# A hybrid decoder on one core: the time mixing's gate is projected ahead of the attention's keys and values, and small products of a step are kept together

## The chip, the core and the metric

The kernel runs on one core of one Trainium2 chip. The metric is the device time of one execution in microseconds (us); a kernel's time is the median of its runs. TensorE (PE) multiplies matrices, VectorE (DVE), ScalarE (ACT) and GpSimd (POOL) work on elements, SyncE (SP) starts the loads of the weights. Each engine executes its own list of instructions in order.

## The reference

Two decoder layers of width 2048 over 256 positions, batch 1, float32. One input projection feeds three token mixers and their gates; their outputs are joined, projected and added to the residual under a layer norm.

```python
u = x @ w_in                     # columns split among the mixers and their gates
# A) short convolution: b * conv3(c * h) * silu(gate)
# B) latent attention: 8 heads, keys/values from ukv (rank 256), queries from uq (rank 512)
# C) time mixing (RWKV-7), 8 heads x 64, gate u_rg:
def step(state, inp):
    r_t, w_t, k_t, v_t, a_t, b_t = inp
    sa = einsum('bhvk,bhk->bhv', state, a_t)
    state = state * w_t + sa * b_t + v_t * k_t
    return state, einsum('bhvk,bhk->bhv', state, r_t)
yf = scan(step)                  # then a norm per head
ym = mean(yf, -1); yv = mean(square(yf - ym), -1)
y = (yf - ym) * rsqrt(yv + eps) * gn_g + gn_b
y = (y + bonus) * silu(gate)
x = LayerNorm(alpha * x + concat(A, B, C) @ w_out)
```

## The kernel before

Every large product is made three times, from a high and a low part of both operands (`mm3`, lines 332 to 334). Weights come in blocks of 1 MB by SP; ACT casts the high part `hi_*` and DVE subtracts to get the low part `lo_*`. A group of the input projection (`in_group`) is 192 matmuls of 128x256 into two accumulators `u_*` of the pool `pp`, which has four. The groups are named k, r, a, v (time mixing), cq (queries' rank), cc, ch, cb, cg (convolution), rg (the time mixing's gate) and mg0, mg1 (the attention's gate). A layer runs the groups of `MAIN`, then `mla_kv` (accumulators pkn and pvt, evicted as kn, vs, vt), `mla_q` (pqn, pqp), then the groups of `LATE`, then the output projection `po`. `plan` lists the weight loads in the same order.

The three mixers are generators. After each small block of a projection, `tick` lets them issue their next steps, so that their small products stand between large ones. The time mixing works in four chunks c of 64 positions: GpSimd and DVE scale keys into `bk` (GpSimd the upper 64 rows, "hi"), TensorE forms the products `pg`, DVE masks them into `gs`, a triangular solve follows (pz, px), and then the recurrence: for each chunk prh from the state, `rhs` on DVE, pu, its copy `uvt` on DVE and ACT, pst, the new state `st` on DVE. `py` gives the outputs of two chunks. When both are there, the norm runs: copies of y on ACT, mean `gm`, difference, squares `gsq`, variance `gv`, a reciprocal root `grs` in small steps, product. Then the transposes `pt`, the activation `yy`, bonus, gate, and the cast `mr` that the output projection reads.

A scheduler puts the instructions of each engine in order when the program is built, by its own estimate of times and by priorities; `tc.high_priority(AHEAD)` moves a step ahead. A tile of a pool is claimed in the order in which the program asks for it (`s8`, nine tiles of 8 KB a partition, holds kn, vs, qn and mr among others).

Of the kernel before, what the change touches and what calls it, by code (L numbers as in the profile page):

```python
# [10 lines left out]
F32 = mybir.dt.float32  # L11
# [98 lines left out]
def hybrid_layers(ctx: ExitStack, tc: tile.TileContext, x, positions, xT, w_in, w_out, w_uq, w_ukv, par, wa_in, gb_in,  # L110
# [34 lines left out]
    def after(inst, earlier):  # L145

        tc.add_manual_dep(inst.ins, earlier.ins.name,
                          mybir.DependencyInfo(mybir.DependencyClass.NoSync, mybir.DependencyReason.DATA),
                          reason="loads no earlier than needed")


    cs = cp.tile([P, K_W], F32, tag="cs", name="cs")
# [186 lines left out]
        for i, src in enumerate((hi, lo)):  # L339
            T.matmul(o, ones[:, which * P:which * P + P], src, start=i == 0, stop=i == 1)  # L340

    MAIN, LATE, ORDER = ("k", "r", "a", "v", "cq", "cc", "ch", "cb", "cg"), ("rg", "mg0", "mg1"), (0, 12, 4, 8)

    def plan():

# [64 lines left out]
    def gate(ps2, name):  # L410

        th = sm.tile([P, 2, S], F32, tag="b2", name=f"th_{name}", bufs=3)
        with tc.high_priority(AHEAD):
            A.activation(th, ps2, AF.Tanh, scale=0.5)
        sg = sm.tile([P, 2, S], F32, tag="b2", name=f"sg_{name}", bufs=3)
        with tc.high_priority(AHEAD):
            V.scalar_tensor_tensor(sg, th, 1.0, ps2, ALU.add, ALU.mult)
        return sg


    UNITS = [(h, c) for c in range(4) for h in range(HEADS)]
# [130 lines left out]
    def rwkv_scale(l, pq, st):  # L552
        col = pq["col"]
        kx, kkn, rx, tha, pe, pinv = (st[k] for k in ("kx", "kkn", "rx", "tha", "pe", "pinv"))
        kp = s4(f"kp{l}")
        for b in range(4):
            A.activation(kp[:, b, :], tha[:, b, :], AF.Identity, scale=col(pq["hk"] + b), bias=col(pq["ok"] + b))
        V.tensor_tensor(kp, kp, kx, ALU.mult)
        V.tensor_scalar(tha, tha, 0.5, 0.5, ALU.mult, ALU.add)
        yield  # L560
        bk = s8(f"bk{l}", (P, 16, P))
        ar = s8(f"ar{l}", (P, 4, 2, S))
        c16 = lambda a: a.rearrange("p b (c t) -> p (b c) t", t=64)
        lo_, hi_ = halves
        G.tensor_tensor(bk[hi_, :, 0:64], c16(kp)[hi_], c16(pinv)[hi_], ALU.mult)
        for b in range(4):
            V.scalar_tensor_tensor(chunks(ar[:, b, 0, :]), chunks(kkn[:, b, :]), -1.0,
                                   pe[:, b * 4:(b + 1) * 4, 0:64], ALU.mult, ALU.mult)
            if b % 2:
                yield  # L570
        V.tensor_tensor(kkn, kkn, tha, ALU.mult)
        G.tensor_tensor(bk[hi_, :, 64:128], c16(kkn)[hi_], c16(pinv)[hi_], ALU.mult)  # L572
        yield
        V.tensor_tensor(bk[lo_, :, 0:64], c16(kkn)[lo_], c16(pinv)[lo_], ALU.mult)
        V.tensor_tensor(bk[lo_, :, 64:128], c16(kp)[lo_], c16(pinv)[lo_], ALU.mult)
        yield
        for b in range(4):
            V.tensor_tensor(chunks(ar[:, b, 1, :]), chunks(rx[:, b, :]), pe[:, b * 4:(b + 1) * 4, 1:65], ALU.mult)
        yield
        st["ar"], st["bk"], st["kp"] = ar, bk, kp  # L580

    def rwkv_v(l, pq, st, uv):
        rx = st["rx"]
# [13 lines left out]
    def rwkv_products(l, st):  # L597

        ar, bk = st["ar"], st["bk"]
        gs = [s8(f"gs{l}_{i}", (P, 2, HEADS, P)) for i in range(2)]  # L600
        for c in range(4):
            cc = slice(c * 64, (c + 1) * 64)
            pg = [pm.tile([P, 4, P], F32, tag="m", name=f"pg{l}_{c}_{par}") for par in range(2)]
            for b in range(4):
                for par in range(2):
                    r = halves[par]
                    T.matmul(pg[par][:, b, :].rearrange("p (q t) -> p q t", q=2), bk[r, b * 4 + c, :], ar[r, b, :, cc],
                             start=True, stop=True)
            for par in range(2):
                gv = gs[c // 2][:, c % 2].rearrange("p (b q) t -> p b q t", q=2)[:, :, par, :]  # L610
                st["mark"] = V.tensor_tensor(gv, pg[par], gmask.unsqueeze(1).to_broadcast([P, 4, P]), ALU.mult)
            yield
        st["gs"] = gs
        col, rx, kp = params[l]["col"], st["rx"], st["kp"]
        for b in range(4):
            V.scalar_tensor_tensor(rx[:, b, :], rx[:, b, :], col(Q_RK + b), kp[:, b, :], ALU.mult, ALU.mult)
        yield
        st["rh"], st["rl"] = c4(f"rh{l}", dt=F32R), c4(f"rl{l}", dt=F32R)
        split_in(st["rh"], st["rl"], rx)

    def rwkv_inverse(l, st):
# [40 lines left out]
        yield  # L662
        for par in range(2):
            r = slice(par * 64, par * 64 + 32)
            V.transpose(xt1[r].rearrange("p c b t -> p (c b) t"), xq[r, :, :, 0:32].rearrange("p c b t -> p (c b) t"))
        yield
        zs = sm.tile([P, 16, 32], F32, tag="s", name=f"zs{l}")
        quarters = [(slice(par * 64, par * 64 + 32), slice(par * 64 + 32, par * 64 + 64)) for par in range(2)]
# [1 line left out]
        for c in range(4):  # L670
            for b in range(4):
                for par, (ra, rb) in enumerate(quarters):
                    T.matmul(pz[par][rb, c * 4 + b, :], gs[c // 2][ra, c % 2, 2 * b + par, 32:64], xt1[ra, c, b, :],
                             start=True, stop=True)
        for par, (ra, rb) in enumerate(quarters):
            V.tensor_copy(zs[rb], pz[par][rb])
        yield
        px = [pm.tile([P, 16, 32], F32, tag="m", name=f"px{l}_{par}") for par in range(2)]
        for c in range(4):
            for b in range(4):  # L680
                for par, (ra, rb) in enumerate(quarters):
                    T.matmul(px[par][ra, c * 4 + b, :], zs[rb, c * 4 + b, :], xq[rb, c, b, 32:64], start=True, stop=True)
        for par, (ra, rb) in enumerate(quarters):
            V.tensor_copy(xq[ra, :, :, 32:64].rearrange("p c b t -> p (c b) t"), px[par][ra])
        yield
        st["xq"] = xq

    def rwkv_pairs(l, st):
# [14 lines left out]
        for b2 in range(2):  # L703
            pv = pm.tile([P, 2, 4, 64], F32, tag="m", name=f"pv{l}_{b2}")
            for bb in range(2):
                for c in range(4):
                    for par in range(2):
                        r, o = halves[par], halves[1 - par]
                        T.matmul(pv[o, bb, c, :], vx[r, b2 * 2 + bb, c * 64:(c + 1) * 64], ident[r, r],
                                 start=True, stop=True)  # L710
            for bb in range(2):
                for par in range(2):
                    o = halves[1 - par]
                    A.copy(hv(uvt, o, b2 * 2 + bb, par), pv[o, bb])
            yield
        st["uvt"], st["bkt"] = uvt, bkt
        qs = s4(f"qs{l}", (P, 4, 4, 64))
        for c2 in range(2):
            pq_ = pm.tile([P, 2, 4, 64], F32, tag="m", name=f"pq{l}_{c2}")
            for cc in range(2):  # L720
                c = c2 * 2 + cc
                for b in range(4):
                    for par in range(2):
                        h = 2 * b + par
                        kr = halves[1 - par]
                        T.matmul(pq_[halves[par], cc, b, :], gs[c // 2][kr, c % 2, h, 0:64], uvt[kr, c, h, :],
                                 start=True, stop=True)
# [4 lines left out]
    def rwkv_chain(l, st):  # L732
# [2 lines left out]
        rs = halves  # L735
        state = None

        def out(c2, states):

            py = [pm.tile([P, 4, 64], F32, tag="m", name=f"py{l}_{c2}_{par}") for par in range(2)]  # L740
            for par in range(2):
                for b in range(4):
                    h = 2 * b + par
                    for i, state in enumerate(states):
                        T.matmul(py[par][halves[i], b, :], gs[c2][:, i, h, 64:128], uvt[:, 2 * c2 + i, h, :],
                                 start=b == 0, stop=state is None, skip_group_check=True)
# [12 lines left out]
        for c in range(4):  # L759
# [10 lines left out]
                yield  # L770
            pu = pm.tile([P, 4, 64], F32, tag="m", name=f"pu{l}_{c}")
            for b in range(4):
                for par in range(2):
                    T.matmul(pu[rs[par], b, :], xq[rs[par], c, b, :], rhs[rs[par], b, :], start=True, stop=True)
            for par in range(2):
                dst = uvt[:, c].rearrange("p (b q) t -> p b q t", q=2)[rs[par], :, par, :]
                if par == 0:
                    V.tensor_copy(dst, pu[rs[par]])
                else:
                    A.copy(dst, pu[rs[par]])  # L780
            yield
            if c < 3:
                pst = pm.tile([P, 4, 64], F32, tag="m", name=f"pst{l}_{c}")
                for b in range(4):
                    for par in range(2):
                        h = 2 * b + par
                        T.matmul(pst[rs[par], b, :], bkt[:, c, h, :], uvt[:, c, h, :], start=True, stop=True)
                new = slot("st", f"st{l}_{c}", (P, 4, 64), 2)
                pc_ = pe[:, c::4, 64:65].to_broadcast([P, 4, 64])
                if state is None:  # L790
# [3 lines left out]
                    V.tensor_tensor(new, new, pc_, ALU.mult)  # L794
            before.append(state)
            if c % 2:
                out(c // 2, before[-2:])
            if c < 3:
                state = new
            yield  # L800
# [117 lines left out]
    def mla_kv(l, st):  # L918
# [4 lines left out]
        for h2 in range(4):  # L923
# [3 lines left out]
            for k in range(2):  # L927
# [5 lines left out]
                for t in range(2):  # L933
                    ts_ = slice(t * P, t * P + P)
                    mm3(pv[:, t, :].rearrange("p (b c) -> p b c", b=2), hi[:, k, ts_], lo[:, k, ts_], wv(whi), wv(wlo),
                        k == 0 and t == 0, k == 1)
            with tc.high_priority(AHEAD):
                A.copy(kn[:, 2 * h2:2 * h2 + 2, :], pk)
                of, pv = slice(2 * h2, 2 * h2 + 2), pv.rearrange("p t (b c) -> p t b c", b=2)
                split_in(vs[:, 0, of, :], vs[:, 1, of, :], pv[:, 0])  # L940
# [5 lines left out]
    def mla_q(l, st):  # L946
# [3 lines left out]
        for g in range(4):  # L950
# [3 lines left out]
            for kc in range(4):  # L954
# [3 lines left out]
                    mm3(pn[:, b, :], whi[:, k, b * P:b * P + P], wlo[:, k, b * P:b * P + P],  # L958
                        hi[:, kc, :], lo[:, kc, :], kc == 0 and b == 0, kc == 3)
                mm3(pe_, whi[:, k, 256:384], wlo[:, k, 256:384], hi[:, kc, :], lo[:, kc, :], kc == 0, kc == 3)  # L960
            with tc.high_priority(AHEAD):
# [387 lines left out]
```

## Time and profile before

| | us |
|---|---|
| median of 3 runs | 933.12 |
| lowest, highest | 930.76, 933.73 |
| the profiled execution | 930.57 |
| its span in the trace | 928.8 |
| PE busy in it | 910.0 |
| DVE, ACT, POOL busy | 682.1, 468.2, 42.0 |

Times in the rows of the profile are measured from the start of the span, and lie 1.8 us within the execution's own time. A row of the list of waits has the waiting engine and its product, the line, what was waited for, then the total in us, how often, and the longest. A row of the stretches has the bounds, the length, then the busy time of PE, PE's weight loads, DVE, ACT and POOL with the number of instructions, the granted clock of TensorE, the share of busy DMA engines, and GB/s. A row of the chain or the timeline has start, duration and what ran. A row of a tile has shortest, median and longest duration in ns, and the first and last start. The mean clock was 0.996 of full speed.

### The profile page before, as it was taken

What the parts mean: (1) busy time and instruction counts of PE and PEld (TensorE: products, weight loads), DVE (VectorE), ACT (ScalarE), POOL (GpSimd) and SP (SyncE); (2) the same over time, 40 slices, a digit from 0 to 9 for tenths busy, and PEclk for the clock granted to TensorE, in tenths of its full rate; (3) what the DMA queues carried; (4) which work ended last, traced back from release to release, by engine and by line L of the source; (5) the groups of instructions that cost most, each with busy time, mean ns of one, the idle gap of its engine ahead of it and who ended that gap; (6) DMA issues with size and microseconds to landing.
All of it is one profiled execution on the core that took longest, in us unless ns stands there. A gap on an engine that the chain in (4) does not pass through costs nothing.

```text
span 928.8 us, 18409 instructions
## 1 busy us (share of the span) xinstructions
PE 910.0 (98%) x7719; PEld 867.6 (93%) x7719; DVE 682.1 (73%) x1132; ACT 468.2 (50%) x716; POOL 42.0 (5%) x47
## 2 busy tenths in 40 slices
PE   8999999999999999999999999999999999999996
PEld 7999989999989999888899999899998999998895
DVE  6687898886569875666766688988854898755665
ACT  6656535543455675434346465463434657754430
POOL 1210130000000000000010001300000000000000
PEclk9999999999999999999999999999999999999999
DMA  8965355354425435964665544463544363259542
GB/s 295 288 200 181 137 187 165 127 183 137 163 98 188 176 127 170 345 208 149 204 227 182 178 148 175 148 203 136 183 117 137 135 225 141 97 175 371 177 136 90
DMA packets 47523, 165.12 MB, mean 178 GB/s; under 512 B 13446, under 2 KB 22198, under 8 KB 32582
## 3 DMA queue, kind: packets, MB, share of 16 engines
q1 hardware_dynamic: 39680, 150.35, 47.4%
q10 hardware_dynamic: 5072, 9.57, 3.3%
q0 software_dynamic: 2688, 4.03, 1.6%
q8 instruction: 60, 0.98, 0.4%
q14 instruction: 23, 0.19, 0.1%
HBM read 158.61 MB, written 5.32 MB: 177 GB/s over the span
## 4 chain that ended last, share of the span: by engine, by line
PE 89%; DMA 3%; DVE 3%; POOL 2%; ACT 1%; issue 1%; SPq 0%; DVEq 0%; ACTq 0%
PE po L332 6%; PE po L333 6%; PE po L334 6%; PE u_mg L334 3%; PE u_mg L333 3%; PE u_mg L332 3%; PE u_ch L332 2%; PE u_cg L333 2%; PE u_cc L332 2%; PE u_cg L332 2%; POOL bk L572 2%; PE u_cg L334 2%; PE u_rg L334 2%; PE u_rg L333 2%; PE u_rg L332 2%; PE u_cb L334 2%
## 5 line engine op out<-in xcount | busy, mean ns | idle before, releaser
L136 DVE TENSOR_TENSOR lo_wo<-w_wo,hi_wo 128x1024 fp32r<-128x1024 f32 x57 | 69.4, 1223 | 51.7 <-ACT hi_wo L136 50.3
L136 ACT CAST hi_wo<-w_wo 128x1024 fp32r<-128x1024 f32 x57 | 59.8, 1053 | 80.8 <-PE po L334 56.0
L333 PE MATMUL u_mg<-x,hi_mg 128*128 128x256 f32 x256 | 72.6, 283 | 0.0
L334 PE MATMUL u_mg<-x,lo_mg 128*128 128x256 f32 x256 | 72.6, 283 | 0.0
L332 PE MATMUL u_mg<-x,hi_mg 128*128 128x256 f32 x256 | 72.4, 283 | 0.0
L136 DVE TENSOR_TENSOR lo_mg<-w_mg,hi_mg 128x1024 fp32r<-128x1024 f32 x32 | 39.1, 1223 | 18.5 <-ACT hi_mg L136 18.4
L333 PEld LDWEIGHTS u_mg<-x,hi_mg 128*128 128x128 f32 x256 | 49.1, 192 | 0.0
L334 PEld LDWEIGHTS u_mg<-x,lo_mg 128*128 128x128 f32 x256 | 49.0, 192 | 0.0
L332 PEld LDWEIGHTS u_mg<-x,hi_mg 128*128 128x128 f32 x256 | 49.0, 192 | 0.0
L333 PE MATMUL po<-lo_wo,ma 128*128 128x512 f32 (+1 forms) x128 | 46.4, 362 | 0.0
L334 PE MATMUL po<-hi_wo,ma 128*128 128x512 f32 (+1 forms) x128 | 46.4, 362 | 0.0
L332 PE MATMUL po<-hi_wo,ma 128*128 128x512 f32 (+1 forms) x128 | 45.9, 363 | 0.0
L136 ACT CAST hi_mg<-w_mg 128x1024 fp32r<-128x1024 f32 x32 | 33.6, 1049 | 22.1 <-PE u_mg L333 13.3
L332 PE MATMUL u_ch<-x,hi_ch 128*128 128x256 f32 x128 | 37.0, 289 | 0.0
L333 PE MATMUL u_cg<-x,hi_cg 128*128 128x256 f32 x128 | 37.0, 289 | 0.0
L334 PE MATMUL u_cq<-x,lo_cq 128*128 128x256 f32 x128 | 37.0, 289 | 0.0
L332 PE MATMUL u_k<-x,hi_k 128*128 128x256 f32 x128 | 36.5, 290 | 0.4 <-ACT hi_k L136 0.3
L333 PE MATMUL u_cq<-x,hi_cq 128*128 128x256 f32 x128 | 36.7, 287 | 0.0
L332 PE MATMUL u_cc<-x,hi_cc 128*128 128x256 f32 x128 | 36.7, 289 | 0.0
L332 PE MATMUL u_cq<-x,hi_cq 128*128 128x256 f32 x128 | 36.6, 286 | 0.0
L332 PE MATMUL u_cg<-x,hi_cg 128*128 128x256 f32 x128 | 36.6, 286 | 0.0
L334 PE MATMUL u_k<-x,lo_k 128*128 128x256 f32 x128 | 35.6, 285 | 0.9 <-DVE lo_k L136 0.9
(424 smaller groups left out, 3417.2 us busy)
## 6 DMA issues: line engine op xcount, KB each, us to landing
w_wo<-in_w_out_dram SPq DMA_DIRECT2D x24, 1024.0 KB, 6.1
w_mg<-in_w_in_dram SPq DMA_DIRECT2D x16, 1024.0 KB, 4.8
w_r<-in_w_in_dram SPq DMA_DIRECT2D x8, 1024.0 KB, 6.4
w_a<-in_w_in_dram SPq DMA_DIRECT2D x8, 1024.0 KB, 4.9
w_v<-in_w_in_dram SPq DMA_DIRECT2D x8, 1024.0 KB, 4.9
w_cq<-in_w_in_dram SPq DMA_DIRECT2D x8, 1024.0 KB, 4.8
w_cc<-in_w_in_dram SPq DMA_DIRECT2D x8, 1024.0 KB, 4.9
w_ch<-in_w_in_dram SPq DMA_DIRECT2D x8, 1024.0 KB, 5.2
```

The source lines that it names most:

```text
L136: inst = call(*args, **kwargs)
L332: m = T.matmul(o, lh, rh, start=first, stop=False, skip_group_check=True)
L333: T.matmul(o, lh, rl, start=False, stop=False, skip_group_check=True)
L334: T.matmul(o, ll, rh, start=False, stop=last, skip_group_check=True)
L572: G.tensor_tensor(bk[hi_, :, 64:128], c16(kkn)[hi_], c16(pinv)[hi_], ALU.mult)
```

## The change

The gate group rg goes from `LATE` to the end of `MAIN`, and with it its four loads. The first matmul of a small product now waits in the order (without a semaphore) for the step's last input, so that the product's matmuls are not spread (`gather`; the two halves of the partitions are taken in the order 1, 0 in pg, pu and pst). GpSimd's two products of 64x1024 into bk become eight of 64x256. `gate` writes into the tile of the tanh. The evictions of mla_kv and mla_q get the priority 4000 in place of 1500.

```diff
+EVICT = 4000
+    def gather(m, earlier):
+        for e in earlier:
+            after(m, e)
-    MAIN, LATE, ORDER = ("k", "r", "a", "v", "cq", "cc", "ch", "cb", "cg"), ("rg", "mg0", "mg1"), (0, 12, 4, 8)
+    MAIN, LATE, ORDER = ("k", "r", "a", "v", "cq", "cc", "ch", "cb", "cg", "rg"), ("mg0", "mg1"), (0, 12, 4, 8)
...
-        sg = sm.tile([P, 2, S], F32, tag="b2", name=f"sg_{name}", bufs=3)
-            V.scalar_tensor_tensor(sg, th, 1.0, ps2, ALU.add, ALU.mult)
-        return sg
+            V.scalar_tensor_tensor(th, th, 1.0, ps2, ALU.add, ALU.mult)
+        return th
...
-        G.tensor_tensor(bk[hi_, :, 0:64], c16(kp)[hi_], c16(pinv)[hi_], ALU.mult)
+        def chunk(c, src, at):
+            cc = slice(c * 64, c * 64 + 64)
+            return G.tensor_tensor(bkc[hi_, :, c, at:at + 64], src[hi_, :, cc], pinv[hi_, :, cc], ALU.mult)
+        for c in range(3):
+            chunk(c, kp, 0)
...
-        G.tensor_tensor(bk[hi_, :, 64:128], c16(kkn)[hi_], c16(pinv)[hi_], ALU.mult)
+        for c in range(4):
+            if c == 2:
+                chunk(3, kp, 0)
+            ready_.append([chunk(c, kkn, 64)])
...
-                for par in range(2):
+                for par in (1, 0):
+                    if b == 0 and par:
+                        gather(m, st["ready"][c])
...
-                for par in range(2):
-                    T.matmul(pu[rs[par], b, :], xq[rs[par], c, b, :], rhs[rs[par], b, :], start=True, stop=True)
+                for par in (1, 0):
+                    m = T.matmul(pu[rs[par], b, :], xq[rs[par], c, b, :], rhs[rs[par], b, :], start=True, stop=True)
+                    if c == b == 0 and par:
+                        gather(m, [st["xq1"]])
...
-            with tc.high_priority(AHEAD):
+            with tc.high_priority(EVICT):
                 A.copy(kn[:, 2 * h2:2 * h2 + 2, :], pk)
```

The same form of `gather` stands in pz, px, pq, pst and py. The built program has 6523 rows on TensorE where it had 6539, the same matmuls.

How the order moves, first on TensorE in layer 0 around the transposes of the time mixing's output. Before, they stand behind the gate's last matmuls (u_rg) and the first of the attention's gate (u_mg), and ahead of the attention's scores (sc):

```order
L333 MATMUL u_rg_1_3524<-x_3_85,hi_rg_12_2_3743 128x256
L334 MATMUL u_rg_1_3524<-x_3_85,lo_rg_12_2_3744 128x256
L332 MATMUL u_mg_0_4047<-x_0_82,hi_mg_0_0_3873 128x256
L333 MATMUL u_mg_0_4047<-x_0_82,hi_mg_0_0_3873 128x256
L334 MATMUL u_mg_0_4047<-x_0_82,lo_mg_0_0_3874 128x256
L828 MATMUL pt_0_3281<-cs,y_2671 128x128 x4
L828 MATMUL pt_1_3347<-cs,y_2671 128x128 x4
L1006 MATMUL sc_0_3603<-kn_3097,qn_3289 128x128
```

Between py_1's last matmul and these stood 295 rows, the rest of the queries and the whole gate. The same place now, from py_1's last matmul on:

```order
L781 MATMUL py_1_1_3055<-st_2_2971,ar_1321 64x64
L339 MATMUL pvt_1_3443<-lo_ukv_1_0_0_3397,hkv_1653 128x256
L340 MATMUL pvt_1_3443<-hi_ukv_1_0_0_3396,hkv_1653 128x256
L338 MATMUL pvt_1_3443<-hi_ukv_1_0_0_3396,hkv_1653 128x256
L339 MATMUL pvt_1_3443<-lo_ukv_1_0_0_3397,hkv_1653 128x256
L340 MATMUL pvt_1_3443<-hi_ukv_1_0_0_3396,hkv_1653 128x256
L862 MATMUL pt_0_3244<-cs,y_2677 128x128 x4
L862 MATMUL pt_1_3286<-cs,y_2677 128x128 x4
L338 MATMUL pkn_2_3478<-hkv_1653,hi_ukv_2_0_0_3438 128x256
```

Five matmuls of the values stand between py_1 and pt_0; the keys pkn_2 follow. The second layer has the same rows.

ScalarE, the evictions of the keys in layer 0. Before, kn<-pkn_0 and kn<-pkn_1 stand behind a copy of the recurrence (uvt) and weight casts:

```order
L136 COPY uvt_1928<-pu_1_2767 64x4x64
L136 CAST hi_uq_0_0_2_3246<-w_uq_0_0_3240 128x2x384
L136 COPY kn_3097<-pkn_0_3106 128x512
L136 COPY kn_3097<-pkn_1_3153 128x512
L136 COPY y_2671<-py_0_0_2824 128x4x64
```

Now they stand behind the norm and the output of the time mixing:

```order
L137 COPY y_2677<-py_1_1_3055 128x4x64
L137 CAST hi_uq_0_0_2_3514<-w_uq_0_0_3508 128x2x384
L137 ACTIVATE gsq_3134<-y_2677 128x1024
L137 ACTIVATE yy_3243<-pt_0_3244,pars 128x256 x2
L137 ACTIVATE yy_3243<-pt_1_3286,pars 128x256 x2
L137 CAST mr_3372<-yy_3243 128x512
L137 COPY kn_3391<-pkn_0_3400 128x512
L137 CAST vs_3393<-pvt_0_3401 128x256
L137 COPY kn_3391<-pkn_1_3442 128x512
```

The squares gsq, the activations yy and the first cast mr have moved ahead of kn<-pkn_0.

VectorE, the norm in layer 0, which stood spread among weight splits. Now one split lo_uq stands between its first two links and the rest follow one another:

```order
L137 TENSOR_REDUCE gm_3130<-y_2677 128x16
L137 TENSOR_TENSOR lo_uq_0_0_2_3515<-w_uq_0_0_3508,hi_uq_0_0_2_3514 128x2x384
L137 TENSOR_SCALAR gm_3130<-gm_3130 128x16
L137 TENSOR_TENSOR y_2677<-y_2677,gm_3130 128x1024
L137 TENSOR_REDUCE gv_3164<-gsq_3134 128x16
L137 TENSOR_SCALAR gv_3164<-gv_3164 128x16
L137 TENSOR_SCALAR grs_3166<-gv_3164 128x16
L137 TENSOR_TENSOR nr_g_3168<-grs_3166 128x16
```

Before, 44 rows lay between gm and the product with grs; now 16 do, and but for lo_uq and a MEMSET they are the norm's own.

More of the change, by code (lines that the diff above doesn't have):

```diff
@@ L564, in rwkv_scale @@
         lo_, hi_ = halves
-        G.tensor_tensor(bk[hi_, :, 0:64], c16(kp)[hi_], c16(pinv)[hi_], ALU.mult)
+        bkc = bk.rearrange("p (b c) t -> p b c t", c=4)
+        def chunk(c, src, at):
[3 more added lines that the diff above has]
+            chunk(c, kp, 0)
         for b in range(4):
@@ L571, in rwkv_scale @@
         V.tensor_tensor(kkn, kkn, tha, ALU.mult)
-        G.tensor_tensor(bk[hi_, :, 64:128], c16(kkn)[hi_], c16(pinv)[hi_], ALU.mult)
+        ready_ = []
+        for c in range(4):
+            if c == 2:
+                chunk(3, kp, 0)
+            ready_.append([chunk(c, kkn, 64)])
         yield
@@ L577, in rwkv_scale @@
         for b in range(4):
-            V.tensor_tensor(chunks(ar[:, b, 1, :]), chunks(rx[:, b, :]), pe[:, b * 4:(b + 1) * 4, 1:65], ALU.mult)
+            v = V.tensor_tensor(chunks(ar[:, b, 1, :]), chunks(rx[:, b, :]), pe[:, b * 4:(b + 1) * 4, 1:65], ALU.mult)
         yield
-        st["ar"], st["bk"], st["kp"] = ar, bk, kp
+        st["ar"], st["bk"], st["kp"], st["ready"] = ar, bk, kp, [r + [v] for r in ready_]
     def rwkv_v(l, pq, st, uv):
@@ L604, in rwkv_products @@
             for b in range(4):
-                for par in range(2):
+                for par in (1, 0):
                     r = halves[par]
-                    T.matmul(pg[par][:, b, :].rearrange("p (q t) -> p q t", q=2), bk[r, b * 4 + c, :], ar[r, b, :, cc],
-                             start=True, stop=True)
+                    m = T.matmul(pg[par][:, b, :].rearrange("p (q t) -> p q t", q=2), bk[r, b * 4 + c, :],
+                                 ar[r, b, :, cc], start=True, stop=True)
+                    if b == 0 and par:
+                        gather(m, st["ready"][c])
             for par in range(2):
@@ L611, in rwkv_products @@
                 st["mark"] = V.tensor_tensor(gv, pg[par], gmask.unsqueeze(1).to_broadcast([P, 4, P]), ALU.mult)
+            if c < 2:
+                st["ready"][c + 2].append(st["mark"])
             yield
@@ L664, in rwkv_inverse @@
             r = slice(par * 64, par * 64 + 32)
-            V.transpose(xt1[r].rearrange("p c b t -> p (c b) t"), xq[r, :, :, 0:32].rearrange("p c b t -> p (c b) t"))
+            t1 = V.transpose(xt1[r].rearrange("p c b t -> p (c b) t"), xq[r, :, :, 0:32].rearrange("p c b t -> p (c b) t"))
         yield
@@ L672, in rwkv_inverse @@
                 for par, (ra, rb) in enumerate(quarters):
-                    T.matmul(pz[par][rb, c * 4 + b, :], gs[c // 2][ra, c % 2, 2 * b + par, 32:64], xt1[ra, c, b, :],
-                             start=True, stop=True)
+                    m = T.matmul(pz[par][rb, c * 4 + b, :], gs[c // 2][ra, c % 2, 2 * b + par, 32:64],
+                                 xt1[ra, c, b, :], start=True, stop=True)
+                    if c == b == par == 0:
+                        gather(m, [t1])
         for par, (ra, rb) in enumerate(quarters):
-            V.tensor_copy(zs[rb], pz[par][rb])
+            z1 = V.tensor_copy(zs[rb], pz[par][rb])
         yield
@@ L681, in rwkv_inverse @@
                 for par, (ra, rb) in enumerate(quarters):
-                    T.matmul(px[par][ra, c * 4 + b, :], zs[rb, c * 4 + b, :], xq[rb, c, b, 32:64], start=True, stop=True)
+                    m = T.matmul(px[par][ra, c * 4 + b, :], zs[rb, c * 4 + b, :], xq[rb, c, b, 32:64],
+                                 start=True, stop=True)
+                    if c == b == par == 0:
+                        gather(m, [z1])
         for par, (ra, rb) in enumerate(quarters):
-            V.tensor_copy(xq[ra, :, :, 32:64].rearrange("p c b t -> p (c b) t"), px[par][ra])
+            st["xq1"] = V.tensor_copy(xq[ra, :, :, 32:64].rearrange("p c b t -> p (c b) t"), px[par][ra])
         yield
@@ L713, in rwkv_pairs @@
                     o = halves[1 - par]
-                    A.copy(hv(uvt, o, b2 * 2 + bb, par), pv[o, bb])
+                    st["uv1"] = A.copy(hv(uvt, o, b2 * 2 + bb, par), pv[o, bb])
             yield
@@ L725, in rwkv_pairs @@
                         kr = halves[1 - par]
-                        T.matmul(pq_[halves[par], cc, b, :], gs[c // 2][kr, c % 2, h, 0:64], uvt[kr, c, h, :],
-                                 start=True, stop=True)
+                        m = T.matmul(pq_[halves[par], cc, b, :], gs[c // 2][kr, c % 2, h, 0:64], uvt[kr, c, h, :],
+                                     start=True, stop=True)
+                        if cc == b == par == 0:
+                            gather(m, [st["uv1"]])
             A.copy(qs[:, c2 * 2:c2 * 2 + 2], pq_)
@@ L736, in rwkv_chain, with out @@
         state = None
-        def out(c2, states):
+        def out(c2, states, moved):
             py = [pm.tile([P, 4, 64], F32, tag="m", name=f"py{l}_{c2}_{par}") for par in range(2)]
@@ L744, in out @@
                     for i, state in enumerate(states):
-                        T.matmul(py[par][halves[i], b, :], gs[c2][:, i, h, 64:128], uvt[:, 2 * c2 + i, h, :],
-                                 start=b == 0, stop=state is None, skip_group_check=True)
+                        m = T.matmul(py[par][halves[i], b, :], gs[c2][:, i, h, 64:128], uvt[:, 2 * c2 + i, h, :],
+                                     start=b == 0, stop=state is None, skip_group_check=True)
+                        if par == b == i == 0:
+                            gather(m, moved)
             for b in range(4):
@@ L772, in rwkv_chain @@
             for b in range(4):
-                for par in range(2):
-                    T.matmul(pu[rs[par], b, :], xq[rs[par], c, b, :], rhs[rs[par], b, :], start=True, stop=True)
+                for par in (1, 0):
+                    m = T.matmul(pu[rs[par], b, :], xq[rs[par], c, b, :], rhs[rs[par], b, :], start=True, stop=True)
+                    if c == b == 0 and par:
+                        gather(m, [st["xq1"]])
+            moved = []
             for par in range(2):
@@ L777, in rwkv_chain @@
                 if par == 0:
-                    V.tensor_copy(dst, pu[rs[par]])
+                    moved.append(V.tensor_copy(dst, pu[rs[par]]))
                 else:
-                    A.copy(dst, pu[rs[par]])
+                    moved.append(A.copy(dst, pu[rs[par]]))
             yield
@@ L784, in rwkv_chain @@
                 for b in range(4):
-                    for par in range(2):
+                    for par in (1, 0):
                         h = 2 * b + par
-                        T.matmul(pst[rs[par], b, :], bkt[:, c, h, :], uvt[:, c, h, :], start=True, stop=True)
+                        m = T.matmul(pst[rs[par], b, :], bkt[:, c, h, :], uvt[:, c, h, :], start=True, stop=True)
+                        if b == 0 and par:
+                            gather(m, moved)
                 new = slot("st", f"st{l}_{c}", (P, 4, 64), 2)
@@ L796, in rwkv_chain @@
             if c % 2:
-                out(c // 2, before[-2:])
+                out(c // 2, before[-2:], moved)
             if c < 3:
@@ L960, in mla_q @@
                 mm3(pe_, whi[:, k, 256:384], wlo[:, k, 256:384], hi[:, kc, :], lo[:, kc, :], kc == 0, kc == 3)
-            with tc.high_priority(AHEAD):
+            with tc.high_priority(EVICT):
                 A.copy(qn[:, 2 * g:2 * g + 2, :], pn)
```

## The prediction

> **What bounds the kernel now.** First the busy times, then the chain of work that ended last, then the waits of TensorE, then busy time by stretch.
>
> ```profile
> PE 910.0 (98%) x7719; PEld 867.6 (93%) x7719; DVE 682.1 (73%) x1132; ACT 468.2 (50%) x716; POOL 42.0 (5%) x47
> PE 89%; DMA 3%; DVE 3%; POOL 2%; ACT 1%; issue 1%; SPq 0%; DVEq 0%; ACTq 0%
> PE prh L767 <- DVE st L136: 3.5, 2, 1.7
> PE pg L607 <- POOL bk L572: 2.7, 2, 1.4
> 110.00:140.00 30.00, 28.63 (x239) 27.33 (x237) 27.95 (x36) 12.13 (x15) 10.65 (x2) 0.94 0.52 178
> 250.00:280.00 30.00, 28.09 (x372) 26.33 (x371) 18.25 (x35) 15.69 (x31) 0.40 (x1) 1.00 0.28 98
> 280.00:300.00 20.00, 20.00 (x169) 20.00 (x168) 19.57 (x37) 13.11 (x19) 0.80 (x3) 1.00 0.60 212
> ```
>
> TensorE (PE) is busy 910.0 of 928.8 us and executes its list in order, so the kernel is its list plus its waits. All waits together are 18.8 us; of these the change can reach only two kinds inside a layer, prh on st (3.5 us in two layers) and pg on bk (2.7 us). Whatever the change gains by taking waits away is therefore under some 7 us; what it may lose has no such bound. The stretch 280 to 300 is to be remembered: TensorE idles for nothing there, while VectorE (DVE) works for 19.57 of 20 us on a chain that nobody waits for yet.
>
> **The gate moved ahead: what loses its cover.** In each layer py closes the recurrence, a norm over y follows on ScalarE (ACT) and DVE, and the transposes pt need its result. Rows of the first layer, from the timeline and the tile views:
>
> ```profile
> 270.21 1.08 PE py L745 x28
> 271.29 0.62 PE py L752 x32
> 272.97 0.65 ACT L136 COPY y<-py 128x256 f32<-128x256 f32 x2
> 274.25 1.21 DVE L136 TENSOR_REDUCE gm<-y 128x16 f32<-128x1024 f32 x1
> 275.38 0.95 DVE L136 TENSOR_TENSOR lo_uq<-w_uq,hi_uq 128x768 fp32r<-128x768 f32 x1
> 276.24 0.17 DVE L136 TENSOR_SCALAR gm<-gm 128x16 f32<-128x16 f32 x1
> 278.63 1.23 DVE L136 TENSOR_TENSOR y<-y,gm 128x1024 f32<-128x1024 f32 x1
> 279.95 1.06 ACT L136 ACTIVATE gsq<-y 128x1024 f32<-128x1024 f32 x1 [1.37 <-DVE y L136]
> 284.42 1.22 DVE L136 TENSOR_REDUCE gv<-gsq 128x16 f32<-128x1024 f32 x1
> 290.46 0.17 DVE L136 TENSOR_SCALAR gv<-gv 128x16 f32<-128x16 f32 x1
> 293.15 0.17 DVE L136 TENSOR_SCALAR grs<-gv 128x16 int32<-128x16 int32 x1
> 302.42 0.18 DVE L136 SCALAR_TENSOR_TENSOR nr_g<-nr_g,gv 128x16 f32<-128x16 f32 x1
> 302.63 0.18 DVE L136 SCALAR_TENSOR_TENSOR grs<-nr_g,grs 128x16 f32<-128x16 f32 x1
> 303.86 1.22 DVE L136 TENSOR_TENSOR y<-y,grs 128x1024 f32<-128x1024 f32 x1
> L828 PE MATMUL pt<-cs,y x16: 272/273/273, 307.3 to 766.4; 128*128 128x128 f32 x16
> ```
>
> Before, py ends at 271.9 and pt starts at 307.3. The 35 us between are filled by the rest of the attention's queries and by the whole gate projection u_rg, so the chain may take its time (it ends at 305.1, with weight splits between its links). In the changed order the gate stands ahead of the keys and values, and between py_1 and pt_0 TensorE has five matmuls left (the first order listing under the change). A matmul of this form issues every 0.12 us (row below), so the cover is 0.6 us.
>
> The chain without strangers, by the rows: two copies of y 0.65; mean 1.21; one lo_uq, which stands in the changed DVE order inside the chain and takes 0.87 until the next starts; 0.17; difference 1.23; squares 1.06; variance 1.22; two small operations 0.34; nine steps of the reciprocal root, which follow each other at 0.21 (302.42 to 302.63), 1.9; product 1.22. That is 9.87 us. Five hand-overs between engines at about 0.1 (278.63 + 1.23 = 279.86, and gsq starts at 279.95) add 0.5, and the end of the last py matmuls 0.1. 10.5 − 0.6 leaves a wait of **9.9 us** at pt_0 in each layer; the order is the same in the second. Bounds: 8.6, if lo_uq slips into the square's 1.06 and hops cost nothing; 10.9, if each hop costs twice.
>
> A second wait follows. In the changed ACT order the first eviction of the keys, kn<-pkn_0, stands behind the four yy<-pt and the first mr<-yy, and pkn_2 needs the accumulator that it frees.
>
> ```profile
> L136 ACT ACTIVATE yy<-pt,pars x8: 557/566/576, 308.5 to 768.1; 128x256 f32<-128x256 f32 x8
> L136 DVE TENSOR_TENSOR yy<-yy,bon x4: 689/690/691, 310.4 to 769.9; 128x512 f32<-128x512 f32 x4
> L136 DVE SCALAR_TENSOR_TENSOR yy<-sg_rg,yy x4: 687/688/690, 313.0 to 772.3; 128x512 f32<-128x512 f32 x4
> L136 ACT CAST mr<-yy x4: 605/606/606, 314.4 to 774.1; 128x512 fp32r<-128x512 f32 x4
> L136 ACT COPY kn<-pkn x8: 586/587/592, 252.1 to 716.4; 128x512 f32<-128x512 f32 x8
> ```
>
> From the end of pt_0: 2 × 0.57 + 0.69 + 0.69 + 0.61 + 0.59 = 3.7, hops 0.3, less the 0.45 in which pt_1 still runs: **3.5 us**. It is 2.9 if the hops vanish and pt takes longer, 4.1 if the next eviction, behind the second mr (0.61), is also waited for. Giving the evictions a higher priority does not help, since mr stands ahead of kn. The last weight splits in the way (hi_ukv, hi_uq) I cost at nothing: they are done while TensorE waits. So are the gate's four weight loads, which SP now issues ahead of those of ukv and uq: in 250 to 280 the DMA engines were 0.28 busy, and the stream that the queue carries is the same one, reordered.
>
> **The clock.** The first layer's short wait at pg was followed by slow matmuls:
>
> ```profile
> 129.20:132.60 3.40, 3.40 (x21) 3.18 (x21) 1.55 (x4) 2.16 (x4) 0.00 (x0) 0.50 0.15 58
> 590.00:594.00 4.00, 4.00 (x48) 3.75 (x48) 2.75 (x5) 2.79 (x5) 0.00 (x0) 1.00 0.00 0
> 129.54 0.22 PE u_cq L334
> 135.28 0.12 PE u_cc L333
> ```
>
> The granted clock was 0.50 for 3.4 us and a matmul took 0.22 instead of 0.12; after the second layer's equal wait (590 to 594) it was 1.00. One throttling costs 3.4 / 2 = 1.7 us. A wait seven times as long should not go unpunished; I take **1.7 us** a layer. Bounds are 0 (no throttling, as after the second pg) and 3.4 (one after each of the two waits).
>
> The Trainium skill, page "TensorE: Matmul & The Clock Gate", section "HAM oscillation — how this bites in real kernels", warns of idle gaps above about 3.4 us, after which work starts at half clock and loses half of the throttled time; this speaks against the change, and by it both layers would pay at pt. The trace here shows a throttling after 1.4 us already, and one wait of that length without.
>
> **Products kept together.** Before, pu_0 and pst_0 were cut by a few projection matmuls; gathered, they cost what the uncut ones cost:
>
> ```profile
> 233.86 0.26 PE pu L774 x2
> 234.66 0.60 PE pu L774 x14
> 235.27 0.32 PE u_cg L333
> 246.75 0.61 PE pu L774 x16
> 131.68 2.56 PE pg L607 x32
> 137.31 1.09 PE pg L607 x8
> ```
>
> pu_0 took 235.27 − 233.86 = 1.41, of it 3 × 0.12 for the matmuls inside: 1.05, against 0.61 whole, so −0.44; pst_0 is cut in the same way, together **−0.9**. py_1's separate head goes too, −0.3 by the same price of a cut. The wait prh <- st goes: 36 matmuls (4.3 us) now lie between pst_2 and prh_3, where DVE needs two products with one split between; **−1.75** by its row. Against that pg_0 is now run in two halves, pg_0_1 and then pg_0_0, with three matmuls between, as pg_3 was already: 2 × 1.09 instead of 2.56 / 2 = 1.28, **+0.9**, and 0.2 for the additional change of form, 1.1.
>
> **Chunks of bk.** What GpSimd did before:
>
> ```profile
> L565 POOL TENSOR_TENSOR bk<-kp,pinv x2: 2775/2778/2780, 109.9 to 569.7; 64x1024 f32<-64x1024 f32 x2
> L572 POOL TENSOR_TENSOR bk<-kkn,pinv x2: 8016/8016/8017, 119.7 to 579.5; 64x1024 f32<-64x1024 f32 x2
> L136 DVE TENSOR_TENSOR lo_cq<-w_cq,hi_cq x16: 1208/1222/3430, 96.8 to 579.3; 128x1024 fp32r<-128x1024 f32 x16
> ```
>
> The same product took 2.78 us once and 8.02 once, and one DVE product beside it 3.43 instead of 1.22: they hold each other up. At 2.2 us (3.43 − 1.22) of own time, a chunk of a quarter is 0.55. pg_0 needs five chunks of the eight, which saves 3 × 0.55 = 1.65 if GpSimd gets in as it did; but pg_0 comes eleven matmuls, 1.3 us, earlier. I take the wait at pg as unchanged (**0**); bounds −1.4 (gone) and +2.1 (below).
>
> The Trainium skill, page "SBUF — State Buffer", section "Who interferes with whom", says that a VectorE instruction with two inputs in SBUF contends with a GpSimd one that reads SBUF, and that the holder keeps the shared ports for its whole instruction. The rows agree (8.02 against 2.78). By it eight chunks must win eight gaps instead of two, which is the rival C below.
>
> The gate's in-place product and its tile change no duration; the matmuls are the same in number.
>
> **Sum.** Per layer 9.9 + 3.5 + 1.7 + 1.1 − 0.9 − 0.3 − 1.75 = +13.25; two layers +26.5. On the profiled execution's 930.57 (span 928.8) this gives 957.1; on the median of the runs, 933.12, which lies 2.55 higher, 959.6. I forecast 958.
>
> **The rivals.**
> A, faster: the norm is done by the time TensorE comes to pt. It decides at 10.5 us between py_1 and pt_0, that is 88 matmuls; the order has five. Only if another list ran than the one printed, or py_1 were long done, would this hold. Then 933.1 + 2 × (1.1 − 0.9 − 0.3 − 1.75) = 929.4, and 926.6 with the pg wait gone as well. 0.05.
> B, smaller loss: the wait at pt at its lower bound, no throttling, and kn waited for 2.9: 933.1 + 2 × (8.6 + 2.9 − 1.85) = 952; with kn free when pkn_2 comes, 947. For it speaks the second layer's pg, after which the clock stayed at 1.00. 0.2.
> C, larger loss: GpSimd starves. DVE's list from kkn to its first wait, gs<-pg_0_1, has a split, four ar, half of bk and two splits without a pause; if only the first chunk got in before, four more must follow after that wait begins, 4 × 0.55 = 2.2 where 1.4 were waited, and the 1.3 by which pg_0 comes earlier is waited too: +2.1 a layer, 958 + 4.2 = 962. With both waits throttled (+1.7 a layer) 965. 0.12.
> D, the moves cancel: savings of the merged steps equal the waits. The savings are 2.95 a layer and would have to be four times as large. 0.03.
>
> **How the numbers follow.** The forecast, 955 to 961.5, has 0.6. Measured differences of this kernel below 0.3%, some 2.8 us, can't be told from no change. Faster by more comes from A, 0.04; within it from D and the rest of A, 0.04; slower 0.92. A range of 946 to 965 takes in B and C but for their tails, and leaves out A and D.
>
> **What would show it.** Right: in the list of TensorE's waits a row pt <- DVE y of about 20 us in two times, a row pkn <- ACT kn of 6 to 7 in two times, no row prh <- st; pu and pst of 16 in one piece; a granted clock below 1 just behind each pt. Wrong: pt not waited for, or its wait below 5 us, which would mean that the chain's rows above do not follow each other as the list says; pg's row above 6 us speaks for C.

## The result, and the profile after

The changed kernel takes 954.07 us (median of 4 runs, 952.68 to 958.89) against 932.39 for the kernel before: a ratio of 1.0243, 95% interval 1.0215 to 1.0271. It is slower, by 21.7 us; 958 was forecast, in a range of 946 to 965. Times are medians of undisturbed executions; of one kernel below, the norm behind the queries, two of ten executions took 2608 and 4092 us, and its only profile is of the second, where TensorE was busy for 4083.5 us, for no cause that was found.

TensorE's waits in the profiled execution of the changed kernel (engine, product and line, what was waited for, total us, times, longest), and stretches around the transposes of both layers and around pg:

```profile
PE 914.4 (96%) x7719; PEld 873.2 (92%) x7719; DVE 684.9 (72%) x1132; ACT 468.3 (49%) x716; POOL 45.1 (5%) x59
PE pt L862 <- DVE y L137: 18.8, 2, 9.4
PE pkn L338 <- ACT kn L137: 5.8, 2, 2.9
PE u_k L338 <- ACT hi_k L137: 2.3, 1, 2.3
279.00:289.10 10.10, 0.73 (x5) 0.53 (x5) 7.77 (x18) 2.52 (x4) 0.00 (x0) 0.67 0.24 78
289.10:294.00 4.90, 1.99 (x9) 1.59 (x9) 2.62 (x5) 3.11 (x7) 0.00 (x0) 0.50 0.00 0
294.00:302.00 8.00, 8.00 (x46) 8.00 (x47) 3.49 (x7) 4.25 (x11) 0.00 (x0) 0.66 0.01 3
762.00:766.00 4.00, 1.10 (x5) 0.74 (x4) 3.33 (x6) 3.37 (x9) 0.00 (x0) 0.50 0.00 0
766.00:775.00 9.00, 9.00 (x61) 9.00 (x60) 3.45 (x7) 5.24 (x12) 0.39 (x1) 0.75 0.00 0
110.00:140.00 30.00, 30.00 (x256) 28.73 (x255) 29.16 (x37) 12.47 (x16) 11.46 (x8) 1.00 0.54 181
```

Two rows are new, pt and pkn, each in both layers alike, and two are gone, prh and pg. Behind pt the granted clock is 0.50 in both layers. Around pg (110 to 140) TensorE now idles for nothing, where it lost 1.37 us before, and its clock stays at 1.00 where it was 0.94. The row u_k stands at the start of the execution, where the first weights arrive; the change does not touch it. It is 2.0 longer than in the profiled execution of the kernel before (0.3), which is part of why these two executions, 955.12 and 930.57 us, lie further apart than the medians.

The chain of work that ended last, in the first layer (start, duration, engine, what ran), reads like the forecast's sum (shortened: between gv and the last y nine steps of the reciprocal root are left out, behind pkn_2's first matmuls more of them):

```profile
278.33 0.64 PE py L781 x32
278.98 0.66 ACT y L137 x2
279.66 1.22 DVE gm L137
280.89 0.86 DVE lo_uq L137
281.87 1.24 DVE y L137
283.19 1.06 ACT gsq L137
284.28 1.23 DVE gv L137
287.83 1.24 DVE y L137
289.11 1.13 PE pt L862 x4
290.26 1.03 ACT yy L137 x2
291.31 0.70 DVE yy L137
292.04 0.70 DVE yy L137
292.82 0.62 ACT mr L137
293.44 0.49 ACT kn L137
293.97 0.58 PE pkn L338
294.56 0.21 PE pkn L339
```

From the end of py to the first pt, every link is the norm's, but for lo_uq; TensorE has only the five pvt matmuls meanwhile. Then yy, the gate, mr and kn hold up pkn_2, and a matmul behind that takes 0.21 us where it took 0.12 at full clock.

### The profile page after: what moved, and what is told of

It is laid out like the page before. It is cut to its first block, busy times and chain, and to the rows that moved or that the text cites. A ratio compares the mean times of both kernels' runs of the same rounds, so it can differ in the third digit from the quotient of the medians.

```text
span 953.3 us, 18417 instructions
## 1 busy us (share of the span) xinstructions
PE 914.4 (96%) x7719; PEld 873.2 (92%) x7719; DVE 684.9 (72%) x1132; ACT 468.3 (49%) x716; POOL 45.1 (5%) x59
## 4 chain that ended last, share of the span: by engine, by line
PE 92%; DVE 4%; DMA 2%; ACT 1%; issue 0%; SPq 0%; DVEq 0%; ACTq 0%
PE po L338 5%; PE po L340 5%; PE po L339 5%; PE u_mg L340 3%; PE u_mg L338 3%; PE u_mg L339 3%; PE u_ch L338 2%; PE u_rg L338 2%; PE u_cc L338 2%; PE u_rg L340 2%; PE u_cq L338 2%; PE u_cg L339 2%; PE u_cg L338 2%; PE u_k L340 2%; PE u_cb L340 2%; PE u_cb L339 2%
## 5 line engine op out<-in xcount | busy, mean ns | idle before, releaser
L338 PE MATMUL u_k<-x,hi_k 128*128 128x256 f32 x128 | 36.8, 292 | 2.3 <-ACT hi_k L137 2.3
L338 PE MATMUL u_rg<-x,hi_rg 128*128 128x256 f32 x128 | 37.0, 289 | 0.0
L339 PE MATMUL u_k<-x,hi_k 128*128 128x256 f32 x128 | 36.9, 292 | 0.0
L340 PE MATMUL u_rg<-x,lo_rg 128*128 128x256 f32 x128 | 36.8, 287 | 0.0
L338 PE MATMUL u_cq<-x,hi_cq 128*128 128x256 f32 x128 | 36.6, 286 | 0.0
L339 PE MATMUL u_cg<-x,hi_cg 128*128 128x256 f32 x128 | 36.6, 286 | 0.0
```

The costliest lines, as they stand in the source:

```text
L338: m = T.matmul(o, lh, rh, start=first, stop=False, skip_group_check=True)
L339: T.matmul(o, lh, rl, start=False, stop=False, skip_group_check=True)
L340: T.matmul(o, ll, rh, start=False, stop=last, skip_group_check=True)
```

## The experiments

Theory: the loss is the norm's lost cover, at pt and at the first evictions, with the clock behind it, and the rest of the change wins. Rivals: the gathering and the chunks cost the time; the gate's new place itself costs it, by loads, accumulators or ScalarE's work. Each ratio below is to the kernel before, run beside it on the same chip. The changed kernel was not run again with them: the kernel before took 931.04 to 931.36 us there and 932.39 beside the changed kernel, so a difference to the changed kernel is uncertain by about 1 us.

**The gate late again, everything else of the change kept.**

```diff
-    MAIN, LATE, ORDER = (..., "cg", "rg"), ("mg0", "mg1"), (0, 12, 4, 8)
+    MAIN, LATE, ORDER = (..., "cg"), ("rg", "mg0", "mg1"), (0, 12, 4, 8)
```

> The changed kernel with the gate group back in LATE; everything else of the change stays. Theory (the loss is the norm's lost cover in front of pt, and the gate's place causes it): pt has 280 rows of cover again, no row pt in PE's waits, no half clock there. What the rest of the change wins remains: the pg wait (1.35 a layer), 1.2 a layer for merged steps, the half clock behind the first pg. prh stays waited for (12 matmuls between). About 926 to 928 against 932.4 before. Rival (gathering and the chunks cost the time): above 945.

Measured: 924.85 us against 931.36, ratio 0.9941 (0.9919 to 0.9963). That is 1 us below what was expected. There is no wait at pt, pkn or pg. Nor is there one at prh, which was expected to stay; pst waits for uvt instead, 2.6 us in two. The rest of the change gains 6.5 us, and the gate's place costs all of the loss.

**The gate early alone, in the kernel before.**

```diff
-    MAIN, LATE, ORDER = (..., "cg"), ("rg", "mg0", "mg1"), (0, 12, 4, 8)
+    MAIN, LATE, ORDER = (..., "cg", "rg"), ("mg0", "mg1"), (0, 12, 4, 8)
```

> The kernel before with only the gate group moved into MAIN. In its order 26 matmuls stand between py_1 and pt_0, so 3.1 us of cover for a chain of 10.0: pt waits 6.9 a layer, pkn_2 2.9, clock 2.7, prh goes (-1.75), pg stays. Theory: 932.4 + 2 x 10.75 = about 954. Rival (gathering and the chunks cost the time): 929 to 934.

```profile
PE pt L828 <- DVE y L136: 13.6, 2, 6.8
PE pkn L332 <- ACT kn L136: 5.8, 2, 2.9
PE pg L607 <- POOL bk L572: 2.7, 2, 1.4
```

Measured: 953.72 us, ratio 1.0245 (1.0216 to 1.0274). TensorE's waits of this run show 6.8 a layer at pt where 6.9 was expected: with 26 matmuls of cover in place of five the wait is 2.6 shorter, and 21 matmuls at 0.12 take 2.5 to run. Gathering and chunks are not needed for the loss.

**The keys' tile claimed early.** The order shows kn<-pkn_0 behind mr. To see whether the tile is the reason, one element of kn is written at the end of the recurrence.

```diff
         done.add(f"chain{l}")
+        t["kn"] = s8(f"kn{l}", (P, HEADS, S))
+        V.memset(t["kn"][0:1, 0, 0:1], 0.0)
...
-        kn = s8(f"kn{l}", (P, HEADS, S))
+        kn = st["kn"]
```

> The changed kernel in which the keys' tile kn is claimed at the recurrence's end by writing one element of it (0.06 us on VectorE), before the norm and before mr. In its order kn's copies no longer stand behind mr, and 36 matmuls stand between py_1 and pt_0 in place of five. Theory: no row pkn <- ACT kn; pt waits 10.0 - 4.3 = 5.7 a layer; the clock costs 0.7 less a layer. 954.1 - 2 x (3.7 + 2.9 + 0.7) = about 939.5. Rival (evictions are late for want of priority or of ScalarE's time, not because of the tile): no change, 953 to 955.

TensorE's waits, and ScalarE's timeline behind pt:

```profile
PE pt L864 <- DVE y L137: 10.3, 2, 5.1
PE pqn L338 <- ACT vt L137: 8.8, 2, 4.4
PE pvt L338 <- ACT kn L137: 1.4, 2, 0.7
293.85 0.62 ACT L137 CAST mr<-yy 128x512 fp32r<-128x512 f32 x1 [0.63 <-DVE yy L137]
294.37 1.18 ACT L137 CAST vs<-pvt 128x256 fp32r<-128x256 f32 x4
296.06 1.36 ACT L137 COPY vt<-pvt 128x256 f32<-128x256 f32 x4
```

Measured: 949.26 us, ratio 1.0194 (1.0166 to 1.0223), not 939.5. For kn the mechanism is right: its copies stand ahead of mr, the row pkn on kn is gone, pt waits 5.1 (5.7 expected). But the evictions of the values, vs and vt, still stand behind mr, and the queries pqn wait 4.4 a layer for vt. The wait had moved on to the next tiles. In the built program, calling for kn's tile earlier without writing it changes nothing: the tile goes to whoever writes first in the order of the program. Nor does the priority of the evictions matter: with 1500 in place of 4000 the built program is the same. (The description of the kernel above says that a tile is claimed in the order in which the program asks for it; this is to be read as the order of first writes.)

**The transposes behind the queries.**

```diff
+        yield from until(f"uq{l}")
         yield
         yy = s4(f"yy{l}")
...
+                    gather(m, [st["behind"]])      # behind: pqp_1's last matmul
```

> The changed kernel in which the transposes pt are issued after the queries and ordered behind the last matmul of the second block of queries (pqp_1), 132 matmuls or 15.8 us behind py_1. Theory: the chain of 10 us is covered, rows pt and pkn vanish from PE's waits, the clock stays at 1.00 there: 954.1 - 2 x (9.4 + 2.9 + 2.7) = about 924, faster than before by the parts of the change that win. Rival (the gate's place itself costs, by weight loads or accumulators): stays above 940 although pt is not waited for.

A row of TensorE's waits, and two of ScalarE's timeline (in brackets, how long it was idle before and what ended that):

```profile
PE pkn L338 <- ACT vt L137: 7.3, 2, 3.7
280.48 1.06 ACT L137 ACTIVATE gsq<-y 128x1024 f32<-128x1024 f32 x1 [1.16 <-DVE y L137]
281.44 0.63 ACT L137 COPY vt<-pvt 128x256 f32<-128x256 f32 x2
```

Measured: 934.42 us, ratio 1.0035 (1.0018 to 1.0052), where 924 was expected: a miss of 10 us, though the rival's 940 is not reached either. pt is not waited for and neither is kn; but pkn waits 3.7 a layer for vt, whose copy starts when the norm's squares gsq have run. gsq and vt come from the same pool (`s4`), and gsq is written first in the program.

**The whole norm behind the queries**, so that it writes nothing ahead of the keys and values.

```diff
+        yield from until(f"uq{l}")
         yield from rwkv_norm(l, pq, t)
```

> The changed kernel in which the whole norm, not only its transposes, is issued after the queries, so that neither the squares gsq nor mr takes a tile ahead of the keys and values. In its order vt<-pvt_0 stands ahead of gsq on ScalarE and pt about 480 rows behind py_1. Theory (tiles are given out in the program's order of first writes, and what the norm writes first holds up the evictions): no row pt, no row pkn, no half clock there: 934.4 of the run with pt behind the queries, less its pkn wait and its clock, 2 x (3.65 + 2.7) = about 922. Rival (the gate's place needs the accumulators or the evictions too late whatever the tiles): stays above 931.

Measured: 925.92 us, ratio 0.9939 (0.9918 to 0.996), where 922 was expected and the rival asked for more than 931. The time agrees with the norm's first writes being what held the evictions; which of its waits went is not shown, since only the times are used.

**The transposes behind the queries, and vt claimed by a write.**

```diff
         done.add(f"chain{l}")
+        t["vt"] = s4(f"vt{l}", (P, HEADS, P))
+        V.memset(t["vt"][0:1, 0, 0:1], 0.0)
... # vt = st["vt"] in mla_kv, and the edit of the run with pt behind the queries
```

> The run with pt behind the queries, in which the values' tile vt is also claimed at the recurrence's end by writing one element of it (0.06 us on VectorE). In its order vt<-pvt_0 has moved from behind gsq to ahead of the copies of y; nothing else moves on TensorE. Theory: the wait of 3.65 a layer of pkn on vt goes, and with it the half clock behind it: about 922. Rival (it was ScalarE's work, not the tile, that made vt late): 934 as without it.

```profile
PE 908.7 (99%) x7719; PEld 866.8 (94%) x7719; DVE 682.4 (74%) x1134; ACT 467.7 (51%) x716; POOL 44.0 (5%) x59
PE pvt L338 <- ACT kn L137: 1.4, 2, 0.7
PE pvt L338 <- ACT vt L137: 0.4, 2, 0.2
276.83 0.37 ACT L137 COPY vt<-pvt 128x256 f32<-128x256 f32 x1 [0.49 <-DVE vs L137]
280.77 1.06 ACT L137 ACTIVATE gsq<-y 128x1024 f32<-128x1024 f32 x1 [0.54 <-DVE y L137]
```

Measured: 925.5 us, ratio 0.995 (0.9935 to 0.9966); 922 was expected. vt's copy now starts at 276.8, four us ahead of gsq, and pkn's wait of 3.7 has shrunk to 0.9 at pvt. One element written moved 8 to 9 us (by the ratios and by the times). With pt and these tiles in order, the early gate is no faster than the late one (924.85): pst's wait of 2.6 is gone, and 1.8 at pvt stand in its place.

**GpSimd's whole products in the changed kernel.**

```diff
... # the product on kp in the same way
-        for c in range(4):
-            ...
-            ready_.append([chunk(c, kkn, 64)])
+        whole = G.tensor_tensor(bk[hi_, :, 64:128], c16(kkn)[hi_], c16(pinv)[hi_], ALU.mult)
+        ready_ = [[whole] for c in range(4)]
```

> The changed kernel with GpSimd's two whole products for bk in place of the eight chunks. TensorE's order is the same. If the chunks removed the wait at pg: pg comes 1.3 us earlier than before the change and waits for the whole of bk, 1.4 + 1.3 = 2.7 a layer, and the first layer is throttled for 1.7 again: 954.1 + 2 x 2.7 + 1.7 = about 961. If the wait went because VectorE comes to its own wait at pg earlier and lets GpSimd in: 954.

```profile
PE pg L619 <- POOL bk L583: 6.2, 2, 3.1
129.20:134.00 4.80, 4.80 (x20) 4.13 (x19) 3.05 (x5) 0.00 (x0) 0.00 (x0) 0.50 0.13 53
570.00:620.00 50.00, 46.90 (x366) 45.72 (x365) 36.49 (x44) 20.21 (x25) 10.78 (x2) 0.90 0.41 138
```

Measured: 966.89 us, ratio 1.039 (1.037 to 1.041), 12.8 more than the changed kernel, where 961 was expected. The wait at pg is 3.1 a layer, not 2.7, and the clock drops behind it in both layers and not in the first alone: 6.2 of waiting, and 6.6 that are left for the clock. The chunks remove the wait at pg, and more than was there before, since the other edits bring pg forward.

**Matmuls in the gaps.** The changed kernel with 36 added matmuls behind py_1 and 10 behind pt_1, whose results nobody reads.

```diff
+        fill(36, st["py"])        # T.matmul(pz, ones[:, 0:P], hkv, ...), 128x512
...
+        fill(10, m)               # behind pt_1
```

> The changed kernel with idle matmuls (128x512, results unused) in the two gaps: 36 behind py_1 (about 8.2 us of the 10.0) and 10 behind pt_1 (2.3 of the 2.9); nothing else changes. It measures the clock alone. Theory (half clock behind each gap costs 2.7 a layer): 954.1 - 5.4 = about 949, with granted clock 1.00 behind pt. Rival (the slow matmuls there come from the evictions, or the fill is too short to hold the clock): 954 or more.

```profile
PE pt L874 <- DVE y L137: 0.7, 2, 0.3
PE pkn L338 <- ACT kn L137: 2.0, 2, 1.0
285.00:305.00 20.00, 18.68 (x137) 17.24 (x136) 14.14 (x30) 11.97 (x24) 0.39 (x1) 1.00 0.27 91
```

Measured: 947.39 us, ratio 1.018 (1.0161 to 1.0199): 6.7 less than the changed kernel (5.9 by the ratios; 949 was expected), with the clock at 1.00 around pt in both layers. The half clock thus cost 3.3 a layer, or 2.9 by the ratios, what pt itself ran slower included. The rest of the loss stands: from the end of py to pt it is 9.6 us here and 10.1 in the changed kernel, so the gap is there when TensorE is kept busy in it too.

**Chunks alone, and gathering without chunks**, both with the gate late.

> The kernel before with only GpSimd's eight chunks for bk; TensorE's and VectorE's orders are those of before. In the changed kernel's trace the chunk that pg_0 needs ended at 122.4, four us ahead of pg_0. If the chunks alone take the wait away: no row pg (2.7) and no half clock behind the first layer's pg (1.7): 931.2 - 4.4 = about 927. If the wait went by the new order around pg instead: 931.

> The kernel with the gate late, the gathered products and the other changes, but with GpSimd's two whole products. If gathering brings pg_0 eleven matmuls earlier onto bk that is not there: pg waits 3.1 a layer and throttles in both layers, as in the run with whole bk and the gate early: 924.9 + 12.8 = about 937.5, slower than before the change. If the interplay needs the early gate: 925 to 929.

```diff
# chunks alone: in the kernel before (the product on kp in the same way)
-        G.tensor_tensor(bk[hi_, :, 64:128], c16(kkn)[hi_], c16(pinv)[hi_], ALU.mult)
+        for c in range(4):
+            if c == 2:
+                chunk(3, kp, 0)
+            chunk(c, kkn, 64)
# gathering without chunks: the first experiment's kernel with the whole products
```

TensorE's waits of the one, with a stretch around prh in the first layer, and of the other:

```profile
PE prh L777 <- DVE st L136: 3.5, 2, 1.7
PE pg L617 <- DVE gs L136: 0.3, 1, 0.3
250.00:280.00 30.00, 28.15 (x317) 26.65 (x316) 18.80 (x35) 15.54 (x28) 0.40 (x1) 0.94 0.29 98
```

```profile
PE pg L619 <- POOL bk L583: 6.2, 2, 3.1
PE pst L815 <- ACT uvt L137: 2.6, 2, 1.3
```

Measured: chunks alone 928.19 us, ratio 0.9965 (0.9949 to 0.998), of which the pg wait of 2.7 is nearly all; 927 was expected. The half clock behind pg is gone too, but in this trace one stretch of it, of 3.4 us, stands behind prh's wait in each layer, where the kernel before had none (1.00 in 250 to 280, with the same wait of 1.7). Gathering without chunks 938.41, ratio 1.0075 (1.0059 to 1.0092), slower than before, with 937.5 expected. Together they gain 6.5: with the chunks, coming early at pg costs nothing, and prh's wait and the cut stretches go, for the 2.6 at pst.

## Why the prediction was right, and where its terms were off

The measured 954.07 lies within the range, but just below the 955 to 961.5 that had a chance of 0.6. The signs that were named came: pt on y 18.8 in two, pkn on kn 5.8 in two (6 to 7 was said), no row prh, pu and pst of 16 in one piece, the clock below 1 behind each pt.

- **Cover of pt**: 9.9 a layer was forecast, 9.4 measured. Right in mechanism and size, down to lo_uq as the one stranger in the chain. The gap follows the cover: 0.6 us of it leaves 9.4, 3.1 leaves 6.8, 4.3 leaves 5.1, and 15.8 leaves nothing. (The upper bound of 10.9 does not follow from its own words: hops at twice the cost add 0.5, which makes 10.4.)
- **pkn on kn**: 3.5 forecast, 2.9 measured. Right, and that priority would not help was right too. From the end of pt_0 to pkn_2 it was 3.7 where 4.0 was forecast, and pt_1, at half clock, covered 0.84 of that and not 0.45. Why mr stands ahead was not said: the order of first writes in the program decides who gets a tile, and the runs with one written element show it for kn and for vt.
- **The clock**: 1.7 a layer forecast, 3.3 measured (2.9 by the ratios), near the upper bound of 3.4. This term of the sum was sized too small. It was taken from one throttling behind one short wait. Here half clock begins within the first gap, at 282.4, where it costs nothing, and lasts to 299.5; in the second layer it is as long, 753.5 to 770.5. pt_0 runs in it, in 1.13 us where it took 0.64 with the gaps filled, and after the second gap it lasts on for 24 matmuls at 0.21. Half of the 5.5 us from 294.0 to 299.5 and the 0.5 of pt_0 make 3.2, an estimate from the trace that agrees. The Trainium skill, page "TensorE: Matmul & The Clock Gate", section "HAM oscillation — how this bites in real kernels", says that a gap above about 3.4 us throttles in every pass of a loop. The trace agrees for the gap of 9.4 us in both layers (granted clock 0.50 behind it). Shorter waits are not safe here: half clock stands behind one of 1.4 in the kernel before and behind the two of 1.7 in the run with chunks alone.
- **pg**: 0 forecast, with −1.4 as the lower bound, and here the forecast was wrong by the most: the wait went altogether, 1.35 a layer, and the first layer's half clock with it. The forecast had seen that pg_0 needs five of the eight chunks, but gave the other three 0.55 each, 1.65 in all, which pg's coming 1.3 earlier would nearly use up. The products of 64x256 on kp and on kkn, from GpSimd's timeline and the tile view of the changed kernel:

```profile
110.98 4.56 POOL L574 TENSOR_TENSOR bk<-kp,pinv 64x256 f32<-64x256 f32 x4 [58.93 <-DVE kp L137]
120.77 6.90 POOL L574 TENSOR_TENSOR bk<-kkn,pinv 64x256 f32<-64x256 f32 x4 [5.24 <-DVE kkn L137]
L574 POOL TENSOR_TENSOR bk<-kkn,pinv x8: 910/1292/3527, 120.8 to 595.4; 64x256 f32<-64x256 f32 x8
```

  The first chunk on kkn ended at 122.4 and the last at 127.7, so the three that pg_0 does not need took 5.2 us and not 1.65. The whole product before had ended at 127.7 as well: GpSimd is done no earlier, but pg_0, at 125.7, no longer waits for all of it. In each layer the fourth chunk on kkn was held up (3.53 in the first). The rival C, starving, did not come, but it was not far: in the run with chunks alone the first chunk on kkn took 6.40 in the first layer and ended at 125.2, as pg_0 began.
- **prh, pu, pst, py**: prh's wait went, as forecast (3.5 in two). The merged steps came as forecast too, by their rows: pu_0 and pst_0 take 0.61 and 0.62 in one piece, py_1 1.72 in place of 2.08, and pg_0's halves 1.08 and 1.09. Their worth in time was not measured apart: the late gate with chunks and gathering gains 6.5, chunks alone 2.9.
- **The sum**: 18.8 + 5.8 + 6.7 lost makes 31.3; 21.7 were measured, so 9.6 were won, of which pg 2.7, prh 3.5 and the first layer's clock 1.7 make 7.9; the rest no run separates. Forecast were 30.2 lost and 3.7 won. The losses came 1.1 above the forecast (the clock 3.3 more, the two waits 2.2 less), the gains 5.9 above it; the difference, 4.8, is what separates 21.7 from the forecast's 26.5. That the total came as near is in part luck: with the clock priced as measured and all else as it stood, the forecast would have been 8.1 too high.

## What to carry to other kernels

Before a projection is moved ahead, look for what it was covering: a chain of small steps that nobody waits for in the profile (busy VectorE, idle nowhere on TensorE) becomes a wait once the matmuls that ran meanwhile are gone, as long as the chain less the cover that is left. Where a shared pool hands tiles out by first write, a step that is issued early but finishes late holds up every eviction behind it, and neither priority nor an earlier call for the tile helps; a later issue, or one written element, does. Price a long gap on TensorE at its length and the half clock after it. And when a consumer waits for a long product of which it needs a part, cut the product: what counts is when that part is done.

## What was not expected of the hardware

GpSimd's products cut into quarters of 64x256 were not faster as a whole. In the changed kernel the four on kp took 4.56 us in the first layer, where the whole product had taken 2.78; the four on kkn took 6.90, where it had taken 8.02, and 9.70 in the run with chunks alone. A single quarter took 0.8 to 1.7 mostly, and up to 6.40.

Half clock came in steps: but for the one that ends each execution, every stretch of it in the traces lasted 3.4, 6.8, 10.2, 13.7 or 17.1 us, multiples of 3.41. And it does not follow a short wait each time: the wait of 1.4 at pg in the kernel before was followed by one stretch in the first layer and by none in the second, the wait of 1.7 at prh by none there and by one in each layer of the run with chunks alone. The kernel's time goes with it: among the 50 executions of the kernel before that ran beside the experiments, the three with a mean clock of 0.998 took 928.5 to 929.5 us, and the eight with 0.991 to 0.993 took 932.2 to 934.5.
